# Moving the operands of a matmul to other addresses: two unused tiles and three earlier requests in a two-layer decoder kernel

## The chip, the cores and the metric

The kernel runs on one core of a Trainium2 chip. The metric is the device time of one execution in microseconds; the median of several runs counts. The matmuls run on TensorE, copies and element-wise work on VectorE and ScalarE, a few small things and some DMA starts on GpSimd, and SyncE starts most DMAs. The profiler records every instruction of these engines with its start and its end.

## What is computed

Two decoder layers over 256 tokens of width 2048, all in float32. Each layer is a token mixer and a gated feed-forward; every part reads a normed copy of the residual stream and adds its own normed result to it. In outline:

```python
def reference(x, mem, norms, w_in_a, w_o_a, g_kv, w_kv, w_in_b, w_o_b,
              w_mem_kv, w_up, w_conv, b_conv, w_down):
    # layer 0
    q, k, v, qm = split(rmsnorm(x, norms[0][0]) @ w_in_a)       # 12 heads of 128, 4 memory heads
    o_dil = three groups of dilated causal attention, merged by their denominators
    o_mem = softmax attention of qm into the 256 rows of mem
    x = x + rmsnorm(concat(o_dil, o_mem) @ w_o_a, norms[0][1])
    x = x + rmsnorm(conv_ffn(rmsnorm(x, norms[0][2])), norms[0][3])
    # layer 1
    k_sh, v_sh = split(rmsnorm(x, g_kv) @ w_kv)
    q, qm = split(rmsnorm(x, norms[1][0]) @ w_in_b)
    o_sb  = stick-breaking attention of q over k_sh, v_sh, 12 heads
    o_mem = softmax attention of qm into mem
    x = x + rmsnorm(concat(o_sb, o_mem) @ w_o_b, norms[1][1])
    x = x + rmsnorm(conv_ffn(rmsnorm(x, norms[1][2])), norms[1][3])
    return x

def conv_ffn(h):                                                # d_ff = 5632
    gate, val = split(h @ w_up)
    return (silu(causal_conv3(gate) + b_conv) * val) @ w_down
```

## The kernel before

**Split operands.** A float32 matrix is used as two parts in the type fp32r: `hi`, a copy (L659 for weights, on ScalarE), and `lo`, what the copy left out (L660, on VectorE). A product is the sum of `hi*hi`, `lo*hi` and `hi*lo`. So each product of the reference is three products of TensorE into the same bank of PSUM.

**Two kinds of matmul.** A matmul loads a stationary tile of 128 x 128 and streams a moving tile of up to 512 columns past it. In `mm3` (L127 and L128) activations are stationary and weights stream by, 512 columns each time: `hi` with the weights' `whi`, `lo` with `whi`, `hi` with `wlo`. In `ws_mm` (L143 to L152, all on L145) weights are stationary: `whi` with both parts of the activations side by side (512 columns), then `wlo` with their `hi` alone (256 columns). These two always come as a pair, except that the last of a tile's sixteen row blocks has them in the other order.

**Who uses which.** `ws_tile`, `ws_pair`, `ws_beside` and the keys in `mem_kv` use `ws_mm`. `as_mm` uses `mm3` for the value projections (`v_proj`, `mem_v`, `mem_kv`), the output projections (`out_proj`) and the second matrix of the feed-forward (`downs`, and the end of `ffn`). `wide` (L671) uses `mm3` too: it computes a 2 x 2 block product with seven products instead of eight (Strassen's way, in Winograd's form), for which it also needs sums of activations and sums of weights. `wide` runs twelve times: five groups of each layer's feed-forward, and the first eight value heads of each layer (`values`). Between its products it computes one `ws_mm` tile in each of its eight steps, and the order of all of this is pinned as written.

**Where the tiles lie.** All of SBUF is one pool, `sb`. The pool places each tile or ring of tiles behind the one before, in the order in which they are first requested in the program, and rounds each up to 32 bytes per partition. The ones that matter here:

- `sh`: a ring of eleven tiles of 4096 bytes. Attention outputs, feed-forward activations (`room`), values, and, in the second layer's `values`, the sums of activations.
- `x`: 16,384 bytes. The residual stream; while `wide` runs, the same place holds `forms`, the two parts of the sums of weights (L968, L1149, L1226).
- `h1` and `h2`: 32,768 bytes each, a set of normed activations in both parts (`hset`). `h1` also holds the sums of activations in all passes of `wide` but the one of the second layer's `values`, and weights at the very end (`stores`).
- `whi` and `wlo`: rings of four tiles of 4096 bytes, the weights' parts, made from `raw`.
- small ones: `cols` (1856 bytes), `mhalf` and `rm` (8 bytes each), `ident`, `mask`, `strict`, `ones`.

Counted from the beginning of the program, `cols` lies at byte 8320, a multiple of 128. Modulo 128 the tiles begin at:

| tile | begins at, modulo 128 |
|---|---|
| `ident`, `mask`, `strict`, `sh`, `mhalf` | 64 |
| `ones`, `x`, `h1`, `rm` | 96 |
| `h2`, `raw`, `whi`, `wlo` | 0 |

Inside a tile all slices that matmuls use step by a multiple of 512 bytes, so the table holds for them too.

Of the kernel before, what the change touches and what calls it, by code (L numbers as in the profile page):

```python
# [10 lines left out]
F32 = mybir.dt.float32  # L11
# [6 lines left out]
P = 128  # L18
D = 2048
# [26 lines left out]
class Body:  # L46
# [999 lines left out]
    def run(self):  # L1046
        nc, a = self.nc, self.a
        sb = self.sb
        self.cols = sb.tile([P, COL_CONV + 8 * NFT], F32, name="cols")
        self.ident = sb.tile([P, P], F32, name="ident")  # L1050
        self.mask = sb.tile([P, 3, S], F32, name="mask")
        self.strict = sb.tile([P, S], F32, name="strict")
        self.rope = self.sh([P, 4, S])
        load = lambda dst, src: self.tc.keep_in_program_order(nc.sync.dma_start(dst, src))
        nc.scalar.dma_start(self.cols[:, :COL_CONV], a["cols"][:, :COL_CONV])
# [4 lines left out]
            load(self.strict, a["strict"])  # L1060
            load(self.cols[:, COL_CONV:], a["cols"][:, COL_CONV:])

        self.mhalf = sb.tile([P, 2], F32, name="mhalf")
        nc.vector.memset(self.mhalf, -0.5)
        self.ones = sb.tile([P, S], F32, name="ones")
        nc.vector.memset(self.ones, 1.0)
        self.x = sb.tile([P, 2, D], F32, name="x", tag="x", bufs=1)
        self.xout = self.outside.tile([2, P, D], F32, name="xout")

        b = self.bank("s")  # L1070
# [2 lines left out]


        self.memT = self.hset("h1")
        self.rm = sb.tile([P, 2], F32, name="rm")

        def before(pi):
            if pi:
# [18 lines left out]
            self.Rm = self.spread(self.rm, "Rm")  # L1098

        h = self.hset("h2")  # L1100

        def x_quarters(pi):
            for i in ((), (), (0,), (1, 2))[pi]:
                self.load_T(a["xT"], COL_G["a0"], h, i)
# [285 lines left out]
```

## Time and profile before

| | |
|---|---|
| median of three runs | 2185.08 us (2184.94 to 2187.57) |
| span of the profiled execution, first to last instruction | 2182.8 us |
| mean granted TensorE clock in it | 0.999 |
| LDWEIGHTS L145, `ps_s<-h,whi` | x1600, 188 ns mean |
| LDWEIGHTS L128, `ps_g<-whi,sh` | x1488, 188 ns mean |
| bytes moved by DMA | 538.84 MB, 247 GB/s mean |

The page gives no time of the profiled execution besides its span; the median of the runs is 2.3 us above that span.

How to read it: PE is TensorE's matmuls, PEld its weight loads, which run beside the matmuls. In a group, the mean of one is how long one instruction took from its own start to its own end; matmuls overlap, so their starts are closer to each other than that. In the chain of work that ended last, in order of time, a row has its start in us, its length in us, what it was, and how many instructions of that kind followed each other there.

### The profile page before, as it was taken

How to read it: one execution, taken by the hardware profiler on the slowest of the kernel's cores; microseconds unless marked ns; L12 is line 12 of the kernel's file. 1: busy time of each engine (PE TensorE's matmuls, PEld its weight loads, DVE VectorE, ACT ScalarE, POOL GpSimd, SP SyncE). 2: the span in 40 equal slices, each digit the busy share in tenths (PEclk: the TensorE clock that was granted, in tenths of full speed). 3: DMA queues.
4: the chain of work that ended last, by engine and by line, in shares of the span. 5: the costliest groups of instructions: out<-in, count | busy, mean ns of one | idle time of the engine just before them, and what ended most of it. 6: DMA issues, size and time to landing. Idle time of an engine off the chain costs nothing.

```text
span 2182.8 us, 29323 instructions
## 1 busy us (share of the span) xinstructions
PE 2168.7 (99%) x10926; PEld 1826.5 (84%) x10926; DVE 1734.9 (79%) x2350; ACT 1327.8 (61%) x1896; POOL 175.5 (8%) x201
## 2 busy tenths in 40 slices
PE   9999999999999999999999999999999999999998
PEld 7888888888888888888888888878888888888886
DVE  7798867997886868788888977579978868687786
ACT  6666746666665666666675655456665655666563
POOL 0000001010101011010011000010101010110100
PEclk9999999999999999999999999999999999999999
DMA  9886457786979879797788744567969798897974
GB/s 364 255 258 244 172 185 256 221 279 220 297 231 281 262 233 298 223 291 252 260 265 260 253 160 174 190 232 226 277 228 290 228 282 264 238 294 220 290 242 182
DMA packets 111776, 538.84 MB, mean 247 GB/s; under 512 B 11280, under 2 KB 11664, under 8 KB 73488
## 3 DMA queue, kind: packets, MB, share of 16 engines
q1 hardware_dynamic: 75744, 445.66, 56.4%
q0 software_dynamic: 35744, 91.24, 20.8%
q8 instruction: 86, 1.41, 0.3%
q14 instruction: 58, 0.48, 0.1%
q10 hardware_dynamic: 144, 0.06, 0.0%
HBM read 510.17 MB, written 26.74 MB: 246 GB/s over the span
## 4 chain that ended last, share of the span: by engine, by line
PE 98%; issue 1%; DMA 1%; ACT 0%; DVE 0%; POOL 0%; SPq 0%; POOLq 0%; DVEq 0%
PE ps_g L128 41%; PE ps_s L145 26%; PE ps_g L145 15%; PE ps_s L128 12%; PE ps_s L952 1%; PE ps_s L277 1%; PE ps_s L353 0%; PE ps_s L380 0%; DMA sh<-in_uw_dram 0%; DMA raw<-in_wmv_dram 0%; PE ps_s L485 0%; PE ps_s L467 0%; PE ps_s L525 0%; PE ps_s L424 0%; DVE x L559 0%
## 5 line engine op out<-in xcount | busy, mean ns | idle before, releaser
L660 DVE TENSOR_TENSOR wlo<-raw,whi 128x1024 fp32r<-128x1024 f32 (+1 forms) x758 | 854.7, 1150 | 256.0 <-ACT whi L659 250.8
L659 ACT CAST whi<-raw 128x1024 fp32r<-128x1024 f32 (+1 forms) x758 | 742.5, 994 | 402.0 <-PE ps_g L128 171.4
L145 PE MATMUL ps_s<-h,whi 128*128 128x512 f32 x1600 | 573.7, 396 | 0.0
L128 PE MATMUL ps_g<-whi,sh 128*128 128x512 f32 x1488 | 464.4, 393 | 0.4 <-ACT sc L770 0.4
L145 PE MATMUL ps_s<-h,wlo 128*128 128x256 f32 x1600 | 431.4, 280 | 0.0
L145 PEld LDWEIGHTS ps_s<-h,whi 128*128 128x128 f32 x1600 | 300.2, 188 | 63.9
L145 PE MATMUL ps_g<-h,whi 128*128 128x512 f32 x960 | 342.6, 400 | 0.8 <-DVE h L267 0.8
L128 PEld LDWEIGHTS ps_g<-whi,sh 128*128 128x128 f32 x1488 | 277.5, 188 | 58.6 <-ACT sc L770 1.3
L145 PEld LDWEIGHTS ps_s<-h,wlo 128*128 128x128 f32 x1600 | 301.4, 188 | 17.3 <-DVE wlo L660 0.3
L128 PE MATMUL ps_g<-wlo,sh 128*128 128x512 f32 x744 | 291.7, 392 | 0.0
L145 PE MATMUL ps_g<-h,wlo 128*128 128x256 f32 x960 | 259.7, 281 | 0.0
L660 DVE TENSOR_TENSOR x<-sh,x 128x1024 fp32r<-128x1024 f32 x192 | 227.0, 1218 | 0.2 <-ACT x L659 0.2
L128 PE MATMUL ps_g<-whi,h 128*128 128x512 f32 x688 | 215.5, 394 | 0.6 <-ACT whi L659 0.6
L145 PEld LDWEIGHTS ps_g<-h,whi 128*128 128x128 f32 x960 | 178.6, 188 | 39.2 <-DVE h L267 1.1
L659 ACT CAST x<-sh 128x1024 fp32r<-128x1024 f32 x192 | 192.8, 1047 | 1.8 <-DVE sh L705 1.8
L145 PEld LDWEIGHTS ps_g<-h,wlo 128*128 128x128 f32 x960 | 181.2, 189 | 4.5
L155 ACT COPY qk<-ps_s 128x256 f32<-128x256 f32 x96 | 35.8, 373 | 229.9 <-PE ps_s L145 229.9
L128 PEld LDWEIGHTS ps_g<-wlo,sh 128*128 128x128 f32 x744 | 139.7, 188 | 32.4
L128 PE MATMUL ps_s<-x,h 128*128 128x512 f32 x552 | 157.8, 394 | 0.0
L667 POOL DMA_DIRECT2D sh<-in_uw_dram x80 | 98.4, 1229 | 660.0 <-DMA sh<-in_uw_dram 295.6
L128 PE MATMUL ps_g<-x,h 128*128 128x512 f32 x528 | 151.4, 394 | 0.0
L128 PEld LDWEIGHTS ps_g<-whi,h 128*128 128x128 f32 x688 | 121.5, 188 | 25.8 <-ACT whi L659 1.0
(215 smaller groups left out, 2255.2 us busy)
## 6 DMA issues: line engine op xcount, KB each, us to landing
raw<-in_up_dram SPq DMA_DIRECT2D x96, 1024.0 KB, 6.9
raw<-in_dn_dram SPq DMA_DIRECT2D x88, 1024.0 KB, 5.3
raw<-in_uw_dram SPq DMA_DIRECT2D x80, 768.0 KB, 7.7
sh<-in_uw_dram SPq DMA_DIRECT2D x80, 512.0 KB, 8.2
sh<-in_uw_dram POOLq DMA_DIRECT2D x80, 512.0 KB, 10.5
raw<-in_wqk_a_dram SPq DMA_DIRECT2D x24, 1024.0 KB, 5.1
yout<-sh POOLq DMA_DIRECT2D x32, 512.0 KB, 8.6
raw<-in_wo_b_dram SPq DMA_DIRECT2D x16, 1024.0 KB, 4.9
```

The costliest lines, as they stand in the source:

```text
L128: mm = lambda *o, **k: self.pin(self.nc.tensor.matmul(*o, **k))
L145: mm = lambda *o, **kw: self.pin(self.nc.tensor.matmul(*o, **kw))
L155: self.pin(self.nc.scalar.copy(out, b[:, S:]))
L277: self.nc.tensor.transpose(b[:, k * S + t * P:k * S + (t + 1) * P], self.x[:, t, kt * P:(kt + 1) * P], self.ident)
L659: high = self.pin(self.nc.scalar.copy(hi, of))
L660: low = self.pin(self.nc.vector.tensor_sub(lo, of, hi.bitcast(F32)))
L667: self.nc.gpsimd.dma_start(d.rearrange("p (a n) -> p a n", a=2), src[u][:, 1536:].unsqueeze(1).to_broadcast([P, 2, 512]), accum_op=ALU.add)
L952: nc.tensor.transpose(b[:, j * S + t * P:j * S + (t + 1) * P], of[t][:, f:f + P], self.ident)
```

## The change

Three tiles are requested earlier, and two tiles are requested that nothing writes or reads: `gap0`, 16 floats (64 bytes), ahead of the ring `sh`, and `gap1`, 112 floats (448 bytes), behind `h2`. The lines that compute, load or store are the same and stand in the same order. Each tile's place in SBUF follows from the new order of requests.

```diff
         self.cols = sb.tile([P, COL_CONV + 8 * NFT], F32, name="cols")
+        self.mhalf = sb.tile([P, 2], F32, name="mhalf")
+        self.rm = sb.tile([P, 2], F32, name="rm")
         self.ident = sb.tile([P, P], F32, name="ident")
         self.mask = sb.tile([P, 3, S], F32, name="mask")
         self.strict = sb.tile([P, S], F32, name="strict")
+        self.x = sb.tile([P, 2, D], F32, name="x", tag="x", bufs=1)
+        sb.tile([P, 16], F32, name="gap0")
         self.rope = self.sh([P, 4, S])
...
-        self.mhalf = sb.tile([P, 2], F32, name="mhalf")
         nc.vector.memset(self.mhalf, -0.5)
         self.ones = sb.tile([P, S], F32, name="ones")
         nc.vector.memset(self.ones, 1.0)
-        self.x = sb.tile([P, 2, D], F32, name="x", tag="x", bufs=1)
         self.xout = self.outside.tile([2, P, D], F32, name="xout")
...
         self.memT = self.hset("h1")
-        self.rm = sb.tile([P, 2], F32, name="rm")
...
         h = self.hset("h2")
+        sb.tile([P, 112], F32, name="gap1")
```

## The prediction, made before the changed kernel ran

> **What bounds the kernel now.** I read the page's busy lines first, then its chain of work that ended last, then the waits of TensorE.
>
> ```profile
> PE 2168.7 (99%) x10926; PEld 1826.5 (84%) x10926; DVE 1734.9 (79%) x2350; ACT 1327.8 (61%) x1896; POOL 175.5 (8%) x201
> PE 98%; issue 1%; DMA 1%; ACT 0%; DVE 0%; POOL 0%; SPq 0%; POOLq 0%; DVEq 0%
> ```
>
> ```profile
> engine line waited for: us in total, times, longest us
> PE ps_s L277 <- DVE x L559: 2.0, 1, 2.0
> ...
> PE ps_s L277 <- DVE h L267: 0.3, 1, 0.3
> ```
>
> The chain is matmuls for 98% of the span, and the six rows of TensorE's waits (first and last are shown) add up to 5.3 us of 2182.8. So TensorE has its next operands ready all the time, and the span is the sum of 10,926 start-to-start intervals. A change that alters no instruction can act only through these intervals.
>
> The groups name the matmuls that matter; their "mean ns of one" (394 to 400) is a latency that overlaps the next matmul and not an interval.
>
> ```profile
> L145 PE MATMUL ps_s<-h,whi 128*128 128x512 f32 x1600 | 573.7, 396 | 0.0
> L145 PE MATMUL ps_g<-h,whi 128*128 128x512 f32 x960 | 342.6, 400 | 0.8 <-DVE h L267 0.8
> L128 PE MATMUL ps_s<-x,h 128*128 128x512 f32 x552 | 157.8, 394 | 0.0
> L128 PE MATMUL ps_g<-x,h 128*128 128x512 f32 x528 | 151.4, 394 | 0.0
> ```
>
> Intervals come from the chain in order of time: each row has a start, a length and a count of matmuls that followed each other, so length over count is the interval. I sort these rows by how far the two operands' addresses lie apart modulo 128. The addresses follow from the order of the requests: before the change `sh` begins at 64, `x` and `h1` at 96, and `h2`, `whi` and `wlo` at 0, and every slice steps by a multiple of 128.
>
> ```profile
> 52.42 21.77 PE ps_g L128 x96
> 311.25 32.97 PE ps_g L128 x144
> 1041.82 21.97 PE ps_s L128 x96
> 1085.77 16.80 PE ps_g L128 x72
> ```
>
> All four are 512-column matmuls of L128 that stream `whi`/`wlo` (at 0). Rows two and three have `sh` stationary, 64 apart: 32.97/144 = 229.0 ns and 21.97/96 = 228.9 ns. Row four, some 20 us later, is the same line with `h1` stationary, 32 apart: 16.80/72 = 233.3 ns. Row one has `h2` stationary, 0 apart: 226.8 ns. So the distance of the operands does show in the interval, by 2 to 3%, though 0 is not slower than 64 in that stretch.
>
> The matmuls of L145 come in pairs: 512 columns with `whi` stationary, 256 with `wlo`, both 0 apart from `h2` or 32 from `h1`.
>
> ```profile
> 35.64 5.55 PE ps_s L145 x32
> 107.65 2.82 PE ps_s L145 x16
> 216.36 5.66 PE ps_g L145 x32
> 393.47 22.52 PE ps_g L145 x128
> 1137.68 22.49 PE ps_g L145 x128
> 1481.40 22.42 PE ps_g L145 x128
> ```
>
> Length over half the count is the time of a pair: 346.9 ns, 352.5, 353.8, 351.9, 351.4, 350.3. The long rows (x128) lie between the two stretches of 32, the fast one at 35.64 and the slow one at 216.36. The timeline inside the slow stretch shows that its pairs are not alike:
>
> ```profile
> 217.61 0.40 PE L145 MATMUL ps_g<-h,whi 128*128 128x512 f32 x1
> 217.85 0.28 PE L145 MATMUL ps_g<-h,wlo 128*128 128x256 f32 x1
> 217.97 0.40 PE L145 MATMUL ps_g<-h,whi 128*128 128x512 f32 x1
> ```
>
> The pair from 217.61 to 217.97 takes 0.36 us, 0.24 of them the 512 columns, against 0.229 of the 64-apart rows.
>
> **The change part by part.** *The requests.* The diff moves three requests for memory up and adds two tiles that nobody uses. No instruction, DMA, wait or order is added, removed or moved; `mhalf`'s memset, `rm`'s writer and `x`'s loads stay where they were. This costs nothing by itself. Afterwards `cols` (1856 bytes, 64 modulo 128) and two tiles of 32 bytes end at 0, so `x` begins at 0; `gap0` puts `sh` at 64, and `h1` and `h2` follow at 64; `gap1` (448 bytes) puts `raw`, `whi` and `wlo` back to 0. So the change does what its name says, with one exception: where `stores` keeps weights in `h1` or `h2` (L594, L1020), some 155 matmuls end up 0 apart instead of 64 or 32; at 2 to 4 ns either way that is at most 0.6 us and stays out of the sum. `sh` with weights was 64 apart already (2496 matmuls) and gains nothing.
>
> *Stationary activations, L128.* The counts follow from the code: twelve passes of `wide`, eight steps each, in a step 6 matmuls of `h2` with weights, 3 of the sums with weights, 9 of the sums with `x`, 3 of `h2` with `x`; the sums lie in `h1` in eleven passes, in `sh` in one. The 864 + 288 with `x` are the 1080 of the groups above and 72 from `sh`.
>
> ```profile
> 104.86 0.70 PE ps_g L128 x3
> 105.56 0.69 PE ps_s L128 x3
> 106.25 0.70 PE ps_g L128 x3
> 106.95 0.70 PE ps_s L128 x3
> ...
> 110.47 1.40 PE ps_g L128 x6
> ```
>
> The four rows of `x` give 2.79/12 = 232.5 ns (0 apart for the first three rows, 32 for the last). At 229.0: 1152 x 3.5 = 4.0 us less. The row of six is `h2` with weights in `wide`, 0 apart but 233.3 ns, in short runs between other kinds: 576 x 4.3 = 2.5 us less. Weights with `h1` (264 in `wide`, 264 in `mem_kv`, `mem_v` and the last rows of `wo_b`): 528 x 4.3 = 2.3 us less. The 192 of `h2` in the two `v_proj` go from 226.8 ns to 229 at worst, 0.4 us more. Sum: 8.4 us less. No trace shows 64 apart in runs of three to nine with other kinds between, so I take 6 of these 8.4 us, with the ends at 0 and 9.
>
> *Pairs, L145.* There are 1600 + 960 = 2560, at some 351.5 ns (the mean of the three long rows and of 352.5, the row of a step of `wide`), 900 us in all, and none of them is 64 apart before. The nearest rows are those of 64 apart in other patterns, 229.0 ns for 512 columns and, for 256, this one:
>
> ```profile
> 2171.25 2.88 PE L128 MATMUL ps_g<-h,sh 128*128 128x256 f32 x24
> ```
>
> The last of the 24 ends 0.28 us after its start, so (2.88 - 0.28)/23 = 113.0 ns. If both held in the pairs: 342.0 ns, 2560 x 9.5 = 24.3 us less. On the other side, if every pair became as in the slow stretch of 353.8 ns: 2560 x 2.3 = 5.9 us more; if every one became the worst pair of it, 360 ns: 21.8 us more. I take the fast stretch, 346.9 ns: 2560 x 4.6 = 11.8 us less. The reason is the 512-column member: 64 apart, long rows hold 229.0 ns, while in the pair it takes up to 0.24 us; bringing that member alone to 229 and leaving the other at the 0.117 or so that remains gives 346, the fast stretch. That 256 columns gain as well rests on 24 matmuls of another pattern.
>
> *What hides or eats it.* TensorE is the chain, so its gain reaches the end unless another engine is late next. The window of the feed-forward's largest stretch shows the room:
>
> ```profile
> 545.00:1100.00 555.00, 555.00 (x2691) 463.59 (x2690) 441.11 (x537) 339.14 (x452) 54.77 (x58) 1.00 0.85 264
> ```
>
> VectorE is busy for 441 of 555 us there, ScalarE for 339, the DMAs for 0.85, at a clock of 1.00. A TensorE that is 0.8% faster takes 4.4 us of the 114 that VectorE has left. These engines read and write the moved tiles too, but not more slowly for it: splitting into `x` (at 96 now) and into `wlo` (at 0) takes the same time.
>
> ```profile
> L660 DVE TENSOR_TENSOR wlo<-raw,whi 128x1024 fp32r<-128x1024 f32 x658 | 793.3, 1221 | 254.5 <-ACT whi L659 249.4 <-PE ps_s L952 1.8 <-PE ps_s L277 1.6
> L660 DVE TENSOR_TENSOR x<-sh,x 128x1024 fp32r<-128x1024 f32 x192 | 227.0, 1218 | 0.2 <-ACT x L659 0.2
> ```
>
> **Sum.** 2182.8 of the span, less 6.0 and 11.8, is 2165.0; the median of the three times is 2.3 us above this span, for what lies around it and the spread of the runs: **2167.3 us**.
>
> **The rivals.** *The pairs stay (2179.1).* Pairs 0 and 32 apart take the same 350 to 352 ns although L128 tells these two apart by 6.5 ns; so their time may come from the alternation of lengths and not from the distance. Then only the 6 us remain. Against it: within one distance pairs differ by 353.8 to 346.9, so something in how the two loads meet does matter.
>
> *Both members fall to the rows of 64 apart (2154.8).* 2185.1 less 6.0 and 24.3. For it: 24 steady matmuls at 113.0. Against it: another pattern.
>
> *Nothing depends on the distance (2185.1).* The two rows of 229 and 233.3 ns could differ by what else ran.
>
> ```profile
> 1036.07:1085.61 49.54, 49.54 (x219) 40.66 (x218) 38.76 (x54) 33.28 (x55) 4.23 (x8) 1.00 0.76 277
> 1085.61:1102.42 16.81, 16.81 (x74) 13.45 (x73) 15.04 (x20) 7.12 (x11) 3.06 (x6) 1.00 0.70 263
> 52.26:74.03 21.77, 21.77 (x98) 18.02 (x97) 17.90 (x29) 19.16 (x37) 3.42 (x5) 1.00 1.00 313
> ```
>
> VectorE is busy for 78% of the first stretch and 89% of the second, the slower one. But the third, with VectorE at 82%, ScalarE at 88% and the DMAs at 1.00, is the fastest of all, so the load of the others does not order them; the distance does. The Trainium skill, in SBUF — State Buffer, section "Who interferes with whom", speaks for this rival: TensorE's moving read and its weight load have ports of their own, independent of each other, and TensorE waits for nobody. By that rule no interval changes and the time stays at 2185.1. The trace disagrees as far as 229.0 and 233.3 ns go.
>
> *Slower: the pairs settle in the bad meeting (2200.9).* The 0.36 us pair is one of three in the slow stretch now. If 64 apart made it the steady one, 2560 x 8.5 = 21.8 us come on top of the 6 gained. It decides from a mean pair of 355.6 ns on (6.0 + 4.4 us over 2560 is 4.1 ns above 351.5). For it: in the long L128 row 0 apart is faster (226.8) than 64 apart (229.0), so 64 is not the best distance everywhere. Against it: no long row of pairs is above 354.
>
> **How the numbers follow.** Forecast 0.42, pairs stay 0.26, both members 0.13, nothing 0.13, slower 0.06. A measurement of this kernel can tell some 0.2%, 4.4 us, from no change, so faster means below 2180.7. The forecast and "both members" are faster; of "pairs stay" 0.18 is faster and 0.08 within, as its own bounds (0 to 9 us for L128) straddle the line; "nothing" is within. That gives faster 0.72, same 0.22, slower 0.06. The range goes from 2153, below "both members", to 2185, which takes in all of "pairs stay" and half of "nothing"; left out are the slower case, the other half of "nothing", and tails.
>
> **What would show it.** In the chain after: rows of L128 with `h` or `x` at 229 ns, where 233 says that the distance is not the cause; the `sh` rows unchanged at 229; the x128 rows of L145 at 22.2 us (22.5 says pairs stay, 21.9 both, 22.8 and over the slow case); the `v_proj` row of x96 up from 21.77 to 22.0. TensorE's waits should stay near 5 us; if they grow, the gain is taken by another engine. The forecast is wrong if the instructions' order changed with the requests, or if the pairs' interval follows something other than this distance.

## The result and the profile after

The changed kernel takes 2199.74 us (median of five runs, 2199.32 to 2201.9), the kernel before 2185.08 us beside it. The ratio is 1.0068, with a 95% interval of 1.0056 to 1.008: the change costs 14.7 us. It was forecast to win 17.8 us.

The profile page of the changed kernel, its busy line and the engines' shares of the chain that ended last:

```profile
PE 2185.3 (99%) x10926; PEld 1829.4 (83%) x10926; DVE 1737.6 (79%) x2350; ACT 1329.0 (60%) x1896; POOL 175.5 (8%) x201
PE 98%; issue 1%; ACT 0%; DMA 0%; DVE 0%; POOL 0%; POOLq 0%; DVEq 0%; SPq 0%
```

The waits of TensorE in the changed kernel, all there are (line waited for: us in total, times, longest):

```profile
PE ps_s L277 <- DVE x L559: 2.0, 1, 2.0
PE ps_s L1074 <- DVE ones L1069: 1.2, 1, 1.2
PE ps_g L128 <- ACT sc L770: 0.4, 2, 0.2
```

The same 10,926 matmuls, the same chain, and waits of 3.6 us where there were 5.3. TensorE is busy 16.6 us longer with the same work, so the loss is in the start-to-start intervals. The window 545 to 1100 us (busy us and instructions of PE, PEld, VectorE, ScalarE, GpSimd; clock, DMA share, GB/s) says the same:

```profile
545.00:1100.00 555.00, 555.00 (x2668) 459.32 (x2667) 436.13 (x532) 338.25 (x450) 55.01 (x58) 1.00 0.84 260
```

At the same clock 2668 matmuls run in it instead of 2691, 0.9% fewer.

The chain of the changed kernel in order of time (start us, length us, what, how many in a row) shows which ones grew:

```profile
51.54 22.40 PE ps_g L128 x96
...
216.52 5.59 PE ps_g L145 x32
...
311.52 33.60 PE ps_g L128 x144
...
394.34 22.49 PE ps_g L145 x128
...
1048.34 22.40 PE ps_s L128 x96
...
1093.14 16.80 PE ps_g L128 x72
...
1145.54 22.45 PE ps_g L145 x128
...
1490.62 22.49 PE ps_g L145 x128
```

Rows three and five are `sh` with weights, which were to stay as they were: 33.60/144 = 233.3 ns for 229.0, and 22.40/96 = 233.3 for 228.9. The first row (`h2` with weights in `v_proj`) went from 226.8 to 233.3, the sixth (`h1` with weights) kept its 233.3. The long rows of L145 stand at 350.8 to 351.4 ns a pair, as before.

From here on I give distances with a sign and modulo 256: the address of the moving tile less that of the stationary tile, between -128 and +128. Modulo 256 the kernel before has `sh` at 192, `x` and `h1` at 224, `h2` and the weights at 0; the changed one has `x` and the weights at 0 and `sh`, `h1`, `h2` at 64. So the weights lay **+64** from `sh` before and lie **-64** from it now. Modulo 128 the two are the same.

The loss by kinds of matmul, as sums of all start-to-start intervals in the two traces, against the terms of the prediction:

| kind | count | forecast, us | measured, us | distance before, after |
|---|---|---|---|---|
| L128, `sh` with weights | 2496 | 0 | +10.6 | +64, -64 |
| L128, `h2` with weights | 768 | -2.1 | +2.7 | 0, -64 |
| L128, `h1` with weights | 528 | -2.3 | -0.9 | +32, -64 |
| L128, `h1`, `h2` and `sh` with `x` | 1152 | -4.0 | +0.7 | 0 or +-32, -64 |
| L145, pairs | 2560 | -11.8 | +2.1 | 0 or -32, +64 |
| L128, `sh` with weights kept in `h1` | 48 | left out | -0.3 | +32, 0 |

Together +14.9 us; the last matmul starts 14.8 us later (2188.66 for 2173.86). The forecast column is what the prediction worked out; of the 8.4 us of its three L128 terms it counted 6. Most of the loss is the first row, for which the prediction had nothing.

### The profile page after: what moved, and what is told of

Read it like the earlier page. It is cut to its first block, busy times and chain, and to the rows that moved or that the text cites. A ratio compares the mean times of both kernels' runs of the same rounds, so it can differ in the third digit from the quotient of the medians.

```text
span 2197.5 us, 29323 instructions
## 1 busy us (share of the span) xinstructions
PE 2185.3 (99%) x10926; PEld 1829.4 (83%) x10926; DVE 1737.6 (79%) x2350; ACT 1329.0 (60%) x1896; POOL 175.5 (8%) x201
## 4 chain that ended last, share of the span: by engine, by line
PE 98%; issue 1%; ACT 0%; DMA 0%; DVE 0%; POOL 0%; POOLq 0%; DVEq 0%; SPq 0%
PE ps_g L128 41%; PE ps_s L145 26%; PE ps_g L145 15%; PE ps_s L128 12%; PE ps_s L952 1%; PE ps_s L277 1%; PE ps_s L353 0%; PE ps_s L380 0%; DMA sh<-in_uw_dram 0%; PE ps_s L485 0%; PE ps_s L467 0%; PE ps_s L1074 0%; PE ps_s L525 0%; PE ps_s L424 0%; PE ps_s L372 0%
## 5 line engine op out<-in xcount | busy, mean ns | idle before, releaser
L145 PE MATMUL ps_s<-h,whi 128*128 128x512 f32 x1600 | 574.6, 395 | 0.0
L128 PE MATMUL ps_g<-whi,sh 128*128 128x512 f32 x1488 | 470.1, 397 | 0.4 <-ACT sc L770 0.4
L145 PE MATMUL ps_s<-h,wlo 128*128 128x256 f32 x1600 | 433.4, 281 | 0.0
L145 PEld LDWEIGHTS ps_s<-h,whi 128*128 128x128 f32 x1600 | 300.4, 188 | 64.5
L145 PE MATMUL ps_g<-h,whi 128*128 128x512 f32 x960 | 343.6, 400 | 0.0
L128 PEld LDWEIGHTS ps_g<-whi,sh 128*128 128x128 f32 x1488 | 276.7, 187 | 67.0 <-ACT sc L770 1.3
L145 PEld LDWEIGHTS ps_s<-h,wlo 128*128 128x128 f32 x1600 | 300.1, 188 | 16.6 <-DVE wlo L660 0.7
L128 PE MATMUL ps_g<-wlo,sh 128*128 128x512 f32 x744 | 293.7, 395 | 0.0
L145 PE MATMUL ps_g<-h,wlo 128*128 128x256 f32 x960 | 260.6, 282 | 0.0
L660 DVE TENSOR_TENSOR x<-sh,x 128x1024 fp32r<-128x1024 f32 x192 | 227.0, 1219 | 0.5 <-ACT x L659 0.5
L128 PE MATMUL ps_g<-whi,h 128*128 128x512 f32 x688 | 217.3, 397 | 0.0
L145 PEld LDWEIGHTS ps_g<-h,whi 128*128 128x128 f32 x960 | 179.0, 188 | 38.0
L145 PEld LDWEIGHTS ps_g<-h,wlo 128*128 128x128 f32 x960 | 180.6, 188 | 4.5
L155 ACT COPY qk<-ps_s 128x256 f32<-128x256 f32 x96 | 35.7, 372 | 231.2 <-PE ps_s L145 231.2
L128 PEld LDWEIGHTS ps_g<-wlo,sh 128*128 128x128 f32 x744 | 139.4, 187 | 34.2
L128 PE MATMUL ps_s<-x,h 128*128 128x512 f32 x552 | 158.4, 395 | 0.0
L128 PE MATMUL ps_g<-x,h 128*128 128x512 f32 x528 | 151.3, 394 | 0.0
L128 PEld LDWEIGHTS ps_g<-whi,h 128*128 128x128 f32 x688 | 122.0, 188 | 26.2
```

Of the source, the lines that this page charges most:

```text
L128: mm = lambda *o, **k: self.pin(self.nc.tensor.matmul(*o, **k))
L145: mm = lambda *o, **kw: self.pin(self.nc.tensor.matmul(*o, **kw))
L155: self.pin(self.nc.scalar.copy(out, b[:, S:]))
L660: low = self.pin(self.nc.vector.tensor_sub(lo, of, hi.bitcast(F32)))
```

## The experiments

Theory after the result: the interval of a matmul follows the *signed* distance of its operands, modulo 256. Rivals: the loss comes from where a tile lies and not from distances; from the pairs; or from distances modulo 128 with the sign meaning nothing. All kernels differ from the changed kernel, or in one case from the kernel before, in unused tiles alone; none has another instruction or another order. "The sets" are `sh`, `h1` and `h2` together. Each kernel ran once, but for the two at the end (five runs each); beside them the kernel before took 2185.09 us (2184.88, the median of nine, for the last four kernels).

**e1_swap: the signs turned round.** The sets at 448 modulo 512, that is at -64, so that L128 has +64 and L145 -64.

```diff
-        sb.tile([P, 16], F32, name="gap0")
+        sb.tile([P, 112], F32, name="gap0")
...
-        sb.tile([P, 112], F32, name="gap1")
+        sb.tile([P, 16], F32, name="gap1")
```

> The two gaps trade sizes (gap0 112 floats, gap1 16): sh, h1 and h2 begin 64 bytes below a multiple of 512 instead of 64 above it, whi, wlo and x stay where the change put them. Theory, the sign counts: what decides is moving address minus stationary address with its sign, modulo 256 or more. L128 is at plus 64 again, so all its long rows go from 233.3 ns to 229.0 (the x144 row of out_proj from 33.60 us to 33.0, the x96 row of v_proj from 22.40 to 22.0); L145 is at minus 64, its pairs between 349 and 354 ns. Time 2180, from 2174 to 2186. Rival, only the distance modulo 128 counts and the loss is from something else that the new order of tiles brought: nothing changes, 2199.7.

Measured: 2183.73 us. The chain in order of time of e1_swap:

```profile
51.73 21.99 PE ps_g L128 x96
...
311.19 32.97 PE ps_g L128 x144
...
393.52 22.57 PE ps_g L145 x128
...
1085.78 16.48 PE ps_g L128 x72
```

229.0 ns for `sh`, 229.1 for `h2`, 228.9 for `h1`: at +64 the three kinds of stationary tile agree, as at -64 they agreed on 233.3. The unsigned distance of all operands is that of the changed kernel, 64 but for the weights kept in `h1` and `h2`, and the time is 16 us apart. That alone excludes distances without a sign, modulo 128 or 256. The pairs of L145 got slower, to 352.7 ns.

**e2_zero: everything at 0.**

```diff
-        sb.tile([P, 16], F32, name="gap0")
+        sb.tile([P, 128], F32, name="gap0")
...
-        sb.tile([P, 112], F32, name="gap1")
```

> gap0 has 128 floats and gap1 is gone: sh, h1, h2, x, whi and wlo all begin at 0 modulo 512. Theory, signed distance: long rows of L128 settle at 226.7 ns as the x96 row of v_proj did before (x144 row of out_proj 32.7 to 33.0 us), short runs in wide stay near 232, pairs of L145 as h2's before, 351 to 352 ns. Time 2172, from 2165 to 2180. Rival, the place of the tile itself: no reason for a gain over before, 2185 or more.

Measured: 2174.6 us, 10.5 below the kernel before. The chain in order of time of e2_zero, its long rows and then a step of `wide` from a window of it:

```profile
51.69 21.77 PE ps_g L128 x96
...
310.15 32.68 PE ps_g L128 x144
...
392.17 22.52 PE ps_g L145 x128
...
1081.23 16.32 PE ps_g L128 x72
```

```profile
104.14 0.70 PE ps_g L128 x3
104.83 0.68 PE ps_s L128 x3
105.52 0.68 PE ps_g L128 x3
106.20 0.68 PE ps_s L128 x3
```

All three kinds are at 226.7 to 226.9 ns, and the four short rows with `x` at 2.74/12 = 228.3. In the changed kernel these four read

```profile
104.58 0.69 PE ps_g L128 x3
105.27 0.70 PE ps_s L128 x3
105.97 0.70 PE ps_g L128 x3
106.67 0.70 PE ps_s L128 x3
```

(the same window of its chain), 2.79/12 = 232.5 ns, exactly what they took before the change. Not every short row is fastest at 0: the rows of six of `h2` with weights in `wide`, over the whole trace, take 231.8 ns in e2_zero, 229.7 in e1_swap and 233.9 in the changed kernel.

**e3_shift: all distances kept, all places moved.** 64 bytes more ahead of `x`; weights, `x` and sets shift together.

```diff
+        sb.tile([P, 16], F32, name="gapx")
         self.x = sb.tile([P, 2, D], F32, name="x", tag="x", bufs=1)
```

> The changed kernel with 16 more unused floats ahead of x: every tile from x on lies 64 bytes higher, all distances are those of the change. Theory, distance: every row as after, L128 at 233.3 ns (x144 row 33.6 us), 2199.7 within 2 us. Rival, the place of a tile counts (sh at 64 modulo 512 is bad, at 448 good): L128 rows with sh move away from 233.3 by 2 ns or more, time off by 5 us or more.

Measured: 2199.18 us, with `sh` and weights at 233.4 ns (mean of all its intervals). All places have moved by 64 bytes and the rows stay, so the place of a tile by itself falls as a cause.

**e4_192: the other 64.** The sets at 192 modulo 512: L128 has +64 modulo 256, but -192 if a larger power of two is the period.

```diff
-        sb.tile([P, 16], F32, name="gap0")
+        sb.tile([P, 48], F32, name="gap0")
...
-        sb.tile([P, 112], F32, name="gap1")
+        sb.tile([P, 80], F32, name="gap1")
```

> gap0 48 floats, gap1 80: sh, h1 and h2 at 192 modulo 512, so L128 is at minus 192. Theory with a period of 256: minus 192 equals plus 64, L128 rows at 229.0 ns and a time like the swapped gaps', some 2180. With a period of 128 (minus 192 equals minus 64): rows at 233.3 ns, 2199.7. With a period of 512: another value than both, or one of them by chance.

Measured: 2183.56 us. The chain in order of time of e4_192:

```profile
51.61 21.99 PE ps_g L128 x96
...
311.04 32.97 PE ps_g L128 x144
```

The rows of e1_swap again: for this distance 256 is a period, and with e1_swap against the changed kernel 128 is not.

**e5_a to e8_d: the other distances.** Each gives the three sets different places. The edit, with the sizes of e5_a:

```diff
-        sb.tile([P, 16], F32, name="gap0")
+        sb.tile([P, 32], F32, name="gap0")
...
+        sb.tile([P, 56], F32, name="gaph")
         self.memT = self.hset("h1")
...
+        sb.tile([P, 16], F32, name="gap2")
         h = self.hset("h2")
-        sb.tile([P, 112], F32, name="gap1")
+        sb.tile([P, 24], F32, name="gap1")
```

The four sizes (`gap0`, `gaph`, `gap2`, `gap1`) are 8, 32, 32, 56 in e6_b; 24, 48, 24, 32 in e7_c; 40, 56, 56, 104 in e8_d.

> Only the sizes of unused tiles differ from the changed kernel. Weights and x lie at 0 modulo 256, sh at 128, h1 at 96, h2 at 160: in L128 the moving weights lie 128 from sh, minus 96 from h1 and plus 96 from h2. Theory (the interval follows the signed distance modulo 256): no run has shown 128; if two sides of 128 are the same thing, its rows lie between those of 0 (226.9 ns) and of plus 64 (229.0), so ps_g L128 x144 at 32.7 to 33.0 us and a time of 2176 to 2188. Rival 1 (modulo 128 after all, with some other difference between plus and minus 64): exactly the rows of distance 0, 32.68 us for x144. Rival 2 (only 0 is fast, plus 64 an exception): 33.60 us for x144 and about 2194 (2496 times 6.4 ns above 2174.6, and 3 to 4 us for h1 and h2).

> Only the sizes of unused tiles differ from the changed kernel. sh and h2 at 32, h1 at 160, weights and x at 0 modulo 256: L128 with sh and h2 has the weights at minus 32. Theory (signed distance modulo 256, and odd multiples of 32 bytes cost what minus 32 cost in x with sh and h2 before, 233.3 ns): ps_g L128 x144 at 33.60 us, and a time of 2174.6 + 2496 x 6.4 ns = 2190.6, with 2 to 6 us more for h1, h2 and L145: 2190 to 2198. Rival (the place of a tile, not its distance, or a rule of 64 byte lines alone, in which 32 is the same line as 0): 32.68 us for x144 and about 2175.

> Only the sizes of unused tiles differ from the changed kernel. sh at 96, h1 at 32, h2 at 128, weights and x at 0 modulo 256: L128 has the weights at minus 96 from sh, minus 32 from h1, 128 from h2. Theory (signed distance modulo 256, odd multiples of 32 cost about 233.3 ns): ps_g L128 x144 at 33.4 to 33.6 us, time 2188 to 2198. The h2 rows of L128 repeat what sh shows at 128 in the run with sh at 128. Rival (only the unsigned distance modulo 128 counts, 96 being 32): the same rows; rival (rows follow 64 byte lines, 96 being 64): 33.6 as at minus 64.

> Only the sizes of unused tiles differ from the changed kernel. sh at 160, h1 at 128, h2 at 96, weights and x at 0 modulo 256: L128 has the weights at plus 96 from sh, 128 from h1, minus 96 from h2. Theory (signed distance modulo 256; odd multiples of 32 cost about 233.3 ns, plus or minus): ps_g L128 x144 at 33.4 to 33.6 us, time 2188 to 2198. Rival (rows follow 64 byte lines and the sign: plus 96 belongs to plus 64): 32.97 us for x144 and about 2182.

Measured: 2190.6, 2194.13, 2198.09 and 2198.05 us. One row of the chain in order of time from each, e5_a, e6_b, e7_c, e8_d, `sh` with weights at 128, -32, -96, +96:

```profile
310.23 33.47 PE ps_g L128 x144
```

```profile
310.24 33.59 PE ps_g L128 x144
```

```profile
311.55 33.73 PE ps_g L128 x144
```

```profile
311.37 33.60 PE ps_g L128 x144
```

232.4, 233.3, 234.2 and 233.3 ns. For e5_a the theory's guess (between 0 and +64) was wrong, its second rival nearly right: 128 is slow too. e6_b, e7_c and e8_d came as expected in their rows (e7_c 0.13 us above), and the times of e7_c and e8_d just over the upper end. So in long rows of L128 only 0 and +64 are fast, and all else measured costs 232 to 234 ns. The long rows of `h2` (x96) and `h1` (x72) stand at other distances in these four runs and bear it out. At -96, `sh` takes 234.2 ns in e7_c, `h2` 22.49/96 = 234.3 in e8_d and `h1` 16.87/72 = 234.3 in e5_a; at +96 all three take 233.3; at 128 `sh` takes 232.4, `h2` 22.30/96 = 232.3 and `h1` 233.3. The distance orders the rows, to within 1 ns, and not the tile.

The same eight runs sort the pairs of L145. Means of start-to-start intervals over the trace (those above 262 ns, which are waits, left out); the pair is `h2` with `whi` and with `wlo`:

| run | `sh` with weights: distance, ns | pair of L145 with `h2`: distance, 512 + 256 columns, ns |
|---|---|---|
| before | +64, 229.0 | 0, 233.9 + 116.6 = 350.5 |
| after | -64, 233.4 | +64, 232.3 + 119.1 = 351.4 |
| e1_swap | +64, 229.0 | -64, 234.2 + 118.3 = 352.5 |
| e2_zero | 0, 227.0 | 0, 234.4 + 116.9 = 351.3 |
| e5_a | 128, 232.4 | -96, 230.5 + 117.3 = 347.8 |
| e6_b | -32, 233.3 | +32, 229.9 + 118.3 = 348.2 |
| e7_c | -96, 234.2 | 128, 230.6 + 119.7 = 350.3 |
| e8_d | +96, 233.3 | +96, 232.8 + 118.4 = 351.2 |

The pairs do depend on the distance, but in another order, and less: 4.7 ns from best to worst in 350, against 7.2 in 230. The 384 pairs with `h1`, which stand at other distances in the same runs, agree with the table's value for their distance within some 1.3 ns.

**u1_shback and u2_shonly: the ring `sh` alone.** The first puts it back to +64 in the changed kernel; the second puts it to -64 in the kernel before and leaves all other tiles where they were modulo 512.

```diff
 u1_shback, from the changed kernel
-        sb.tile([P, 16], F32, name="gap0")
+        sb.tile([P, 48], F32, name="gap0")
...
+        sb.tile([P, 32], F32, name="gaph")
         self.memT = self.hset("h1")
...
-        sb.tile([P, 112], F32, name="gap1")
+        sb.tile([P, 48], F32, name="gap1")
```

```diff
 u2_shonly, from the kernel before
+        sb.tile([P, 32], F32, name="gapa")
         self.rope = self.sh([P, 4, S])
+        sb.tile([P, 96], F32, name="gapb")
```

> The changed kernel with the ring sh alone moved by 128 bytes, so that the weights lie plus 64 from it modulo 256, as before the change; h1 and h2 stay at 64, x and weights at 0. Theory (the loss is the 2496 matmuls of sh with weights, which went from plus 64 to minus 64): ps_g L128 x144 falls from 33.60 to 32.97 us, and the time by 2496 x (233.4 - 229.0) ns = 11.0 us, from 2199.2 to 2188.2 (2186 to 2191). Rival (the pairs of L145 or the matmuls with h1 and h2 are the loss): 2197 to 2200.

> The kernel before with the ring sh alone moved by 128 bytes, so that the weights lie minus 64 from it modulo 256; every other tile keeps its place modulo 512. Theory: ps_g L128 x144 rises from 32.97 to 33.60 us, and the time by 11.0 us, from 2185.1 to 2196.1 (2194 to 2198). Rival (modulo 128, as the prediction had it): nothing moves, 2185.1.

Measured: 2190.87 and 2195.38 us. The chain in order of time of u2_shonly, and then of u1_shback:

```profile
51.66 21.77 PE ps_g L128 x96
...
310.71 33.60 PE ps_g L128 x144
...
1046.06 22.40 PE ps_s L128 x96
```

```profile
311.97 32.97 PE ps_g L128 x144
...
631.02 11.20 PE ps_g L128 x48
```

`sh` alone takes the kernel before from 2184.88 to 2195.38, +10.5 us (11.0 expected), and its two rows of `sh` to the 233.3 ns of the changed kernel, while the `h2` row in front stays at 226.8. In the other direction 8.3 us come back (from 2199.18, the changed kernel's distances in e3_shift, a single run as well; 8.9 from the changed kernel's median; 11.0 expected). More than half of the missing part shows in the second row of u1_shback: eight such rows of 48, each right behind a pass of `wide`, still take 11.20/48 = 233.3 ns at the same +64 that gives 229.0 in the row of 144. In the kernel before this row is

```profile
629.63 10.98 PE ps_g L128 x48
```

that is 228.8 ns. So a distance of +64 allows both. What ran ahead of these rows is what differs, short rows with `x` and `h1` that are still at -64; that this decides was not tried by itself.

**b1_h2 and z5_zero: what the table is good for.** z5_zero has the distances of e2_zero, in five runs. It has no `gap0` where e2_zero has one of 512 bytes, so its tiles from `sh` on lie 512 bytes lower, at the same places modulo 512. This is not quite "the same kernel", as the expectation below has it, but the time and the rows agree. It is also the change without its two unused tiles: the three earlier requests alone. b1_h2 takes it and moves `h2` alone to 160, where its pairs are at the best distance of the table and its matmuls of L128 at a bad one.

```diff
 b1_h2, from z5_zero
+        sb.tile([P, 40], F32, name="gap2")
         h = self.hset("h2")
+        sb.tile([P, 88], F32, name="gap1")
```

> Everything at 0 modulo 256 but h2, at 160: L145 with h2 then has the sets minus 96 from the weights, and L128 with h2 has the weights and x plus 96 from it. Theory (each class of matmuls adds up by its own distance, with the means of the runs with these distances): against everything at 0, 2176 pairs of L145 with h2 at 347.8 ns for 351.3, -7.6 us; 768 of h2 with weights at 233.4 for 230.7, +2.1; 288 of h2 with x at 232.8 for 226.7, +1.8; sum -3.7, from 2174.6 to 2170.9 (2169 to 2173). Rival (the classes do not add up, since what runs before a pair shifts it): 2173 to 2178.

> Sets, x and weights all at 0 modulo 256, the same kernel that gave 2174.6 us in one look, now timed in five rounds against the kernel before. Expected: 2174.6 again, a ratio of 0.9952 to the kernel before.

Measured: z5_zero 2175.06 us, ratio to the kernel before 0.9957 (0.9944 to 0.9971); b1_h2 2171.44 us, 0.9939 (0.9927 to 0.9952). Both beat both kernels: the three earlier requests by themselves win 0.4%, and the two unused tiles turn that into the loss. Between the two lie 3.6 us where 3.7 were added up from single distances. The chain in order of time of b1_h2 has the gain and the price:

```profile
51.53 22.40 PE ps_g L128 x96
...
309.20 32.68 PE ps_g L128 x144
...
390.83 22.22 PE ps_g L145 x128
```

`h2` with weights went to 233.3 ns, the pair to 22.22/64 = 347.2, and `sh` kept its 226.9.

## Why the prediction was wrong

**What bounds the kernel: right.** No instruction moved, TensorE stayed the chain, its waits did not grow, and the whole difference lies in intervals. That the distance of the operands shows in the interval was right too, so the rival "nothing depends on the distance" falls: e2_zero, e1_swap and the changed kernel run the same instructions and take 2174.6, 2183.73 and 2199.74 us. By the rule of the Trainium skill named there (SBUF — State Buffer, "Who interferes with whom": TensorE's moving read and its weight load have independent ports), as the prediction reads it, they should take the same time; the three times do not agree with that.

**The step that failed** is how rows were sorted: "by how far the two operands' addresses lie apart modulo 128". From it came "`sh` with weights was 64 apart already (2496 matmuls) and gains nothing". These matmuls went from +64 to -64 modulo 256, and they lost 10.6 us of the 14.8; u2_shonly shows that this one move, made alone, costs 10.5 us. The trace of before had no row at -64, so the step should have been treated as unknown, with bounds from the nearest rows: 2496 times anything from 226.8 to 233.3 ns, that is -5.5 to +10.7 us. With no gain elsewhere that puts the upper end of the range at about 2196, and makes a loss far more likely; the last 4 us are the other terms, which turned as well.

**L128 with `h1`, `h2` and `x`, taken as -6 us:** sized by 229.0 ns, the row of +64, for matmuls that came to -64. They settled at 233.3 in long rows and 232.5 in short ones, and the three kinds together gave +2.5 us. In e1_swap, where they are at +64, the long rows of `h1` and `h2` do show the 229 ns. By all their intervals the three kinds are 5.7 us below the kernel before in that run (`h1` -3.0, `h2` -0.5, `x` -2.1), so the sum had about the right size for the other sign. Its term of 2.5 us for `h2` in `wide` was too large all the same: it was read from one row of six at 233.3 ns, and over the whole trace of before these rows take 231.2. The prediction also had the 226.8 ns of 0 apart in hand, noted that 0 was not slower than 64, and still counted the short rows with `x` at 0 apart as a gain to come.

**The pairs, taken as -11.8 us:** they gave +2.1. The reasoning was that 64 apart brings the 512-column member to 229 and leaves the other at 117. The first half went that way in part (233.9 to 232.3, `h2`); the second did not, the 256-column member rose from 116.6 to 119.1. At all distances measured the pair with `h2` stays between 347.8 and 352.5 ns, in the mean over a trace. The forecast of 346.9, read from one row of 32, lies below all of these means. The rival "the pairs stay" had this nearly right.

**The slower rival** (pairs settling at 360 ns) named the right side with the wrong mechanism: the pairs cost 2.1 us and not 21.8. That its 2200.9 lies 1.2 us from the measured time is luck. The chances with the other rivals are added up with a small slip: by their own terms faster comes to 0.73 and same to 0.21, not 0.72 and 0.22. **The change does what it says** modulo 128; the sign was the part of it that its words and the prediction both left out.

## What to carry to other kernels

When fp32r matmuls with a fresh weight load each bound a kernel and hardly ever wait, as here, the addresses of their operands are a parameter worth trying: the same instructions took from 2171.44 to 2199.74 us, 1.3% apart. Here the moving tile at the same address modulo 256 as the stationary one was the best place for 512-column matmuls in long rows, and bringing all of them there gained 0.4%. Measure such a distance with its sign and its true period before sorting rows by it; a case that looks unchanged under the sorting is an unknown if the trace has no row of it. The means of a kind over whole traces with the same distances added up well here (3.6 us measured for 3.7 summed). A value from one kind of row did not carry over to another: the pairs of 512 and 256 columns, and short rows between other kinds, had to be measured in their own right.

## What the runs showed of the hardware

The interval of a 512-column fp32r matmul in long rows of L128, against the signed distance of moving and stationary tile modulo 256: 226.7 to 226.9 ns at 0, 229.0 at +64, and 232.3 to 234.3 at -64, -32, +32, +-96 and 128, all at a granted clock of 0.998 to 0.999. In the row of 144 single intervals run 226, 229, 232 in turn at +64 (before, e1_swap), alternate between 231 and 236 at -64 (after), and are all 226 or 227 at 0 (e2_zero). One distance can hold two steady intervals, as the rows of 48 and of 144 in u1_shback show (233.3 and 229.0 ns at +64).

Why the distance acts is open. By the starts in the traces a weight load of 188 ns begins 2 to 5 ns after nearly every matmul of L128 does, so a load and a matmul run side by side; but whether the distance to the current or to the next stationary tile counts, or something besides these two reads, was not tried. Nor were `whi` and `wlo` at different places, which might suit the pairs and L128 at once.
